# Two shift columns and one row chunk moved between stages of a conditioned convolution block on one Trainium2 core

## The chip, the cores and the metric

The kernel runs on one core of one Trainium2 chip. The metric is the device time of one execution in microseconds (us). Engines are named as in the profile: PE is the matrix engine, PEld its weight load, DVE the vector engine, ACT the scalar engine, POOL the third elementwise engine, SP the engine whose queue issues the transfers from device memory (SPq are its queue's own instructions).

## The reference, cut to what matters

One layer of a block: a modulation of the condition vector, a gated causal depthwise convolution as mixer, and an MLP with a squared ReLU. d is 2048, the sequence 256, the MLP width 8192, the convolution 31 taps.

```python
cond = jax.nn.silu(c)
mod = cond @ mod_w[i] + mod_b[i]
sh1, sc1, g1, sh2, sc2, g2 = jnp.split(mod, 6, axis=-1)
h = _rms_norm(x, norm1_g[i]) * (1.0 + sc1[:, None, :]) + sh1[:, None, :]
y = _conv_mixer(h, ...)   # in-projection to a and gt, u = a * sigmoid(gt), 31 taps per channel,
                          # layer norm over channels, silu, out-projection
x = x + (1.0 + g1[:, None, :]) * y
h = _rms_norm(x, norm2_g[i]) * (1.0 + sc2[:, None, :]) + sh2[:, None, :]
u = jnp.square(jax.nn.relu(h @ mlp_w1[i]))
x = x + (1.0 + g2[:, None, :]) * (u @ mlp_w2[i])
```

All is float32. The six modulation vectors (sh1 to g2) are a matrix-vector product with a 2048 x 12288 matrix, 96 MB of weights that are used once.

## The kernel before

**Tiling.** Channels lie on the 128 partitions in 16 tiles, tokens (256) on the free axis. The weights come in tiles of 128 x 16 x 128 float32 (1024 KB) through one ring of five buffers, the tile `raw` (RAW = 5, line 41). SP issues the loads in the order of the list `order` (lines 489 to 500), each as soon as a buffer of the ring is free (`top_up`, line 164): a load waits for the work that reads the buffer's earlier content.

**Float32 in two parts.** A weight tile is split into a rounded part `hi` (ACT, line 204) and the rest `lo` (DVE or POOL, line 207), in two halves each, by `split_w`; activations likewise by `split_act` (lines 215 to 218). `hi` and `lo` have six half buffers each, so a split also waits for the matmuls of earlier jobs. A product is hi by hi, hi by lo and lo by hi; in the last input job and in the output jobs these are three matmuls of 256 tokens (lines 228 to 230).

**Jobs.** After a first part, in which the SC1 and SH1 columns of the modulation and eight input tiles are computed together, the work is a list of jobs: `in 8` to `in 15` (one pair of tiles of a and gt each), the norm (code behind the last input job, lines 839 to 907), `out 0` to `out 7` (two output tiles each, the residual and the second norm's sums), then the MLP's `up` and `down`. The weights of a job are split one job ahead (`splits(jobs[n + 1])`, line 777), those of `out 1`'s first half already in in 15 (`parts_early`).

**Modulation beside the jobs.** What the later stages need of the modulation is computed in between, by one of two routes:

- a *row chunk* (`mod_chunk`, line 299): four matmuls on PE (line 308) with a slice of the condition as weights. 32 of them make G1 and SC2.
- a *column* (`mod_col`, line 377): DVE multiplies a weight tile of 128 x 2048 by the condition and sums along the free axis (line 388). Within out 1 to out 5 the condition has a copy in PSUM, and the column is done in two halves (line 384). 16 of them make SH2, and 16 others G2.

How many stand behind which job is written by hand in `LATE_IN` (row chunks, line 50) and `LATE_OUT` (SH2 columns, line 51). The six row chunks of in 15 are executed in the norm: the first behind the tokens' sums (`stats_end`), four behind `sum_end`, the last behind `row_end` (lines 854, 870, 896).

**Tile 14 and 15 of the convolution.** Half of the tiles' convolutions are done by DVE, tap by tap (line 622), the others by PE with diagonal weights (line 730, weights by POOL in line 715), from a shifted copy `wide` of the gated input (`copy_wide`, line 698). The copies of tiles 14 and 15 are shared between DVE (line 705, nine of them) and ACT (line 707, seven). The gate that makes their input is line 747.

**Order on an engine.** A planner places the instructions on each engine ahead of time, from the program's order, the marks of `urgent()` and its own estimate of when things are ready; `issue_after` fixes that one instruction stands behind another. On the chip each engine then works through its list in that order. ACT therefore evacuates an output job (line 916) and rounds the next job's weights (line 204) in the order that the planner chose.

Of the kernel before, what the change touches and what calls it, by code (L numbers as in the profile page):

```python
# [17 lines left out]
KT = D // P  # L18
# [16 lines left out]
SH1, SC1, G1, SH2, SC2, G2 = range(6)  # L35

GROUPS = [[4 * w + b for b in range(4)] for w in (G1, SC2)]
ROWS = [nb for g in GROUPS for nb in g]
# [8 lines left out]
COPY_AT = {8: 0, 9: 1, 10: 2, 11: 9, 12: 10, 13: 12}  # L47
PADDING = 784
UNSHIFTED = 7
LATE_IN = [0] * 8 + [4, 4, 4, 4, 4, 3, 3, 6]  # L50
LATE_OUT = [1, 2, 2, 3, 3, 3, 1, 1]
URGENT = 400
HELD = 8
EARLY_U = 5
# [10 lines left out]
def conv_block(ctx: ExitStack, tc: tile.TileContext, x, vec, dwq, c_row, mod_r, mod_c, w_first, w_in, w_out, w1, w2, out):  # L65
    nc = tc.nc
# [49 lines left out]
    state = {"used": 0}  # L116
# [12 lines left out]
    def urgent():  # L129
        return tc.high_priority(offset=URGENT)  # L130
# [89 lines left out]
    def mm(p, c, key, acts_of, ks=range(KT), merged=False):  # L220
        halves = parts[key]
        for k in ks:
            hi, lo = halves[k // HALF]
            m = acts_of[k // 2][:, k % 2, :]
            if merged:
                out_p, begin, end = p[:, c, 0:T], k == 0, k == KT - 1
                w = hi[:, k % HALF, :]
                nc.tensor.matmul(out_p, w, m[:, 0:T], start=begin, stop=False)  # L228
                nc.tensor.matmul(out_p, w, m[:, T : 2 * T], start=False, stop=False)  # L229
                state["mm_end"] = nc.tensor.matmul(out_p, lo[:, k % HALF, :], m[:, 0:T], start=False, stop=end)  # L230
                continue
            nc.tensor.matmul(p[:, c, :], hi[:, k % HALF, :], m, start=(k == 0), stop=(k == KT - 1))  # L232
            state["mm_end"] = nc.tensor.matmul(  # L233
                p[:, c, T : 2 * T], lo[:, k % HALF, :], m[:, 0:T], start=False, stop=(k == KT - 1),
                skip_group_check=True,
            )
# [62 lines left out]
    def mod_chunk(nb, kg):  # L299
        w = take(("mod", nb, kg))  # L300
        group = next(g for g in GROUPS if nb in g)
        b = group.index(nb)
        begin, end = b == 0 and kg == 0, b == len(group) - 1 and kg == 3
        if begin:
            mod_finish()
            row_ps.append(ps.tile([P, 512], F32, name="row", bufs=1))
        for k in range(4):
            state["row_end"] = nc.tensor.matmul(  # L308
                row_ps[0][32 * k : 32 * k + 32, :], cz[:, 4 * kg + k, 3 - b : 35 - b], w[:, 4 * k : 4 * k + 4, :],
                start=begin, stop=end,  # L310
            )
        if end:
            r = tmp.tile([P, 512], F32, name="rowsb", bufs=1)
            with urgent(), tc.issue_after(state["hi_end"]):
                nc.scalar.activation(r, row_ps.pop(), AF.Copy)
            pending.append(([4 * nb for nb in group], 4, r))

    def shift_row(at, w):
        if at == 0:
            row_ps.append(ps.tile([P, 512], F32, name="row", bufs=1))  # L320
        for k in range(KT):
            g = k % 4
            nc.tensor.matmul(
                row_ps[0][32 * g : 32 * g + 32, at * P : (at + 1) * P], shz[:, k, :], w[:, k, :],
                start=(k < 4), stop=(k >= KT - 4),
            )

    def fold_shift():
        n = 2 * UNSCALED
        r = tmp.tile([P, 512], F32, name="rowsb", bufs=1)  # L330
        p = ps.tile([P, 512], F32, name="row", bufs=1)
        with urgent():
            nc.scalar.activation(r[:, 0 : n * P], row_ps.pop()[:, 0 : n * P], AF.Copy)
            for j in range(n):
                nc.tensor.matmul(p[:, j : j + 1], r[:, j * P : (j + 1) * P], col("pick", 0, 1), start=True, stop=True)
            nc.scalar.activation(shc, p[:, 0:n], AF.Copy)
# [40 lines left out]
    def mod_col(at):  # L377
        w = take(("col", at)).rearrange("p k n -> p (k n)")
        which, k = divmod(at, KT)
        acc = modc[:, at : at + 1]  # L380
        if which == SH2 and "cond" in state:
            n = HALF * P
            for half, total in zip(state["cond"], (acc, rest2[:, k : k + 1])):
                nc.vector.scalar_tensor_tensor(w[:, 0:n], w[:, 0:n], 1.0, half, op0=ALU.mult, op1=ALU.mult, accum_out=total)
                w = w[:, n:]
            return
        with tc.issue_after(state["e_end"]) if "e_end" in state else ExitStack():
            nc.vector.scalar_tensor_tensor(w, w, 1.0, cb, op0=ALU.mult, op1=ALU.mult, accum_out=acc)  # L388
        if which in amps:
            return nc.vector.scalar_tensor_tensor(  # L390
                amps[which][:, k : k + 1], acc, col("modb", at), col("n1g", k), op0=ALU.add, op1=ALU.mult
            )
        elif which != SH2:
            return mod_bias(at, 1, acc)

    def mods(keys):
        for key in keys:
            if key[0] == "mod":
                mod_chunk(*key[1:])
            else:  # L400
                mod_col(key[1])
# [28 lines left out]
    def two():  # L430
        return tmp.tile([P, 2, T], F32, name="two", bufs=6)
# [28 lines left out]
        nc.scalar.activation(s, src, AF.Square)  # L460
        return s

    late = [("mod", nb, kg) for nb in ROWS for kg in range(4)] + [("col", SH2 * KT + k) for k in range(KT)]
    last = [("col", G2 * KT + k) for k in range(KT)]

    jobs = [("in", i) for i in range(KT)] + [("out", i) for i in range(HALF)]
# [2 lines left out]
    def by_tokens(job):  # L469
        return job[0] == "down" or job[0] == "up" and job[1:] not in ((0, 0), (0, 1))  # L470

    quota = {("in", i): n for i, n in enumerate(LATE_IN)}
    quota.update({("out", i): LATE_OUT[i] for i in range(HALF)})
    after = {}
    for job in jobs:
        n = quota.get(job, 0)
        after[job], late = late[:n], late[n:]
        if job[:2] in LATE_GATE:
            n = LATE_GATE[job[:2]][job[2]]
            after[job], last = last[:n], last[n:]  # L480
# [217 lines left out]
    def copy_wide(ct, both=True):  # L698
        wides[ct] = cp.tile([P, 4, T + 28], F32, name="wide", bufs=2)
        for q in range(4):  # L700
            for g in range(4):
                dst = wides[ct][32 * q : 32 * q + 32, g, :]
                src = u[ct][32 * g : 32 * g + 32, q : q + T + 28]
                if both and (g % 2 or (q, g) == (3, 2)):
                    nc.vector.tensor_copy(dst, src)
                else:
                    nc.scalar.activation(dst, src, AF.Copy)

# [62 lines left out]
    for n, job in enumerate(jobs):  # L771
# [6 lines left out]
        if n in COPY_AT:  # L778
            with tc.issue_after(state["sg"].ins) if n == HELD else ExitStack():
                copy_wide(COPY_AT[n], False)  # L780
# [3 lines left out]
        kind, i = job[0], job[-1]  # L784
# [7 lines left out]
        if job == ("up", 0, 0):  # L792
            mm(p, 0, job + (0,), xa, range(SIDE))
            for at in range(2 * UNSCALED):
                shift_row(at, shown.pop(("up", 0, at // 2, at % 2)))
            fold_shift()
            mm(p, 0, job + (0,), xa, range(SIDE, KT))
            mm(p, 1, job + (1,), xa)
        elif job in K_OUTER:
            for k2 in range(HALF):  # L800
                for c in range(2):
                    mm(p, c, job + (c,), xa if plain else hl, range(2 * k2, 2 * k2 + 2), kind == "out")
        elif kind == "in":
            rows = list(after[job]) if i < KT - 1 else []
            for c in range(2) if i < KT - 1 else (1, 0):
                for ks in (range(HALF), range(HALF, KT)):
                    mm(p, c, job + (c,), hl, ks, i == KT - 1)
                    with tc.issue_after(state["mm_end"].ins):
                        mods(rows[:1])
                    del rows[:1]  # L810
        elif by_tokens(job):
            mm_tokens(sums[kind, i // 2], job, u2 if kind == "down" else hl, n == len(jobs) - 1)
        else:
            for c in range(2):
                mm(p, c, job + (c,), hl, merged=kind == "out")
        mod_finish()
        if kind == "in":
            with urgent():
                gate(i, evac(p, out=p[:, :, 0:T]) if i < KT - 1 else p[:, :, 0:T])
                if i >= KT - 2:  # L820
                    copy_wide(i)
# [24 lines left out]
                nc.scalar.activation(sq[:, k - 12, :], cv(k), AF.Square)  # L846
            table(AF.Abs_reciprocal_sqrt, sq[:, 2, 0:1])
            sums = two()[:, 0, :]
            rows = list(after[job])
            with urgent(), tc.issue_after(state["conv_end"].ins):  # L850
                sum_round([(cv(k), sq[:, k - 12, :]) for k in (12, 13)], last=(1,))
                sum_round([(cv(14), sq[:, 2, :])], last=(0,))
# [29 lines left out]
            for k2 in range(HALF):  # L882
                e = two()
                f = ps_two()
                with urgent():
                    nc.gpsimd.tensor_tensor(e, pair_of(cvs, k2), spread(mu), op=ALU.subtract)
                    state["e_end"] = nc.vector.tensor_tensor(e, e, spread(r), op=ALU.mult).ins
                    for c in range(2):
                        k = 2 * k2 + c
# [18 lines left out]
        if kind == "out":  # L908
# [4 lines left out]
            with urgent():  # L913
                for c in range(2):
                    k = 2 * i + c
# [10 lines left out]
            for c in range(2):  # L926
                k = 2 * i + c
# [138 lines left out]
```

## Time and profile before

| what | us |
|---|---|
| median of 3 runs | 1111.2 |
| the runs | 1109.98, 1111.20, 1111.62 |
| the profiled execution, its time | 1112.2 |
| the profiled execution, its span (first to last instruction) | 1110.4 |

| engine | busy share of the span |
|---|---|
| PE | 98% |
| PEld | 81% |
| DVE | 67% |
| ACT | 46% |
| POOL | 17% |

A row of a group names the line, the engine, the operation, the tiles written and read (`out<-in`), shapes, a count after x, then busy us and the mean ns of one, then the idle time of the engine in front of them and what ended it. A row of the timeline has start and length in us, engine, line, operation, tiles, shapes, count, and in brackets the idle time before it with its releaser. Times are counted from the span's start. PE counts each float32 matmul of a row chunk and of the convolution twice, so a row chunk of four matmuls is eight instructions of line 308. Idle time of DVE, ACT or POOL costs nothing by itself, as long as PE does not wait for them.

### The profile page before, as it was taken

The numbers are of one execution on the slowest core, as the hardware profiler recorded it, in microseconds if no ns is written. First come the engines' busy times: TensorE is split into PE (matmuls) and PEld (weight loads), VectorE is DVE, ScalarE is ACT, GpSimd is POOL, SyncE is SP. The second block draws the span as 40 slices with busy tenths as digits, with TensorE's granted clock in tenths as the row PEclk, the third lists the DMA queues.
The fourth block names the chain that finished last, engine by engine and source line by source line (L and its number), as shares of the span: only waits on it lengthen the run. The fifth ranks groups of instructions, "written<-read, shape, count | busy, mean of one in ns | idle before, by whom it ended". The sixth has DMA issues, their size and how long they took to land.

```text
span 1110.4 us, 15401 instructions
## 1 busy us (share of the span) xinstructions
PE 1089.3 (98%) x6018; PEld 894.6 (81%) x6018; DVE 745.8 (67%) x1029; ACT 506.9 (46%) x677; POOL 191.7 (17%) x119
## 2 busy tenths in 40 slices
PE   7999999999899999999999999999999999999998
PEld 4888876667599998888888888888888888888887
DVE  5777789987466887666875567644656565565553
ACT  4111386754675477443444444333444344444431
POOL 0000176467679343000000000000000000000000
PEclk8999999999999999999999999999999999999999
DMA  9999989878679967878998889757888977788641
GB/s 384 421 420 422 416 335 355 339 302 344 227 304 390 395 245 252 242 233 272 374 369 290 234 242 295 299 156 261 250 237 236 248 206 226 219 241 250 209 143 38
DMA packets 142315, 314.23 MB, mean 283 GB/s; under 512 B 87585, under 2 KB 105505, under 8 KB 107297
## 3 DMA queue, kind: packets, MB, share of 16 engines
q1 hardware_dynamic: 142096, 313.11, 81.2%
q8 instruction: 47, 0.77, 0.3%
q14 instruction: 26, 0.21, 0.1%
q10 hardware_dynamic: 146, 0.13, 0.0%
HBM read 301.15 MB, written 12.07 MB: 282 GB/s over the span
## 4 chain that ended last, share of the span: by engine, by line
PE 82%; DMA 11%; DVE 4%; SPq 1%; ACT 1%; issue 0%; DVEq 0%; ACTq 0%
PE mm L256 18%; PE mm L257 18%; PE mm L255 18%; DMA raw<-mod_c 9%; PE mm L232 6%; PE mm L233 3%; DVE raw L388 3%; PE acc L230 2%; PE acc L228 2%; PE acc L229 2%; PE row L308 2%; PE mm L730 2%; DMA flat<-two 1%; PE mm L229 1%; SPq L275 1%; DVE lo L207 1%
## 5 line engine op out<-in xcount | busy, mean ns | idle before, releaser
L204 ACT ACTIVATE hi<-raw 128x1024 fp32r<-128x1024 f32 x320 | 333.7, 1056 | 359.7 <-PE mm L257 292.8
L207 DVE TENSOR_TENSOR lo<-raw,hi 128x1024 fp32r<-128x1024 f32 x257 | 311.7, 1222 | 168.4 <-ACT hi L204 168.1
L256 PE MATMUL mm<-lo,u 128*128 128x512 f32 x496 | 193.2, 390 | 0.4 <-DVE lo L207 0.4
L255 PE MATMUL mm<-hi,u 128*128 128x512 f32 x496 | 193.0, 389 | 0.0
L257 PE MATMUL mm<-hi,u 128*128 128x512 f32 x496 | 193.0, 389 | 0.0
L207 POOL TENSOR_TENSOR lo<-raw,hi 128x1024 fp32r<-128x1024 f32 x63 | 152.3, 2445 | 206.3 <-DMA raw<-w_in 132.3
L257 PE MATMUL mm<-hi,hl 128*128 128x512 f32 x480 | 186.7, 389 | 0.0
L256 PE MATMUL mm<-lo,hl 128*128 128x512 f32 x480 | 186.7, 389 | 0.0
L255 PE MATMUL mm<-hi,hl 128*128 128x512 f32 x480 | 186.7, 389 | 0.0
L388 DVE SCALAR_TENSOR_TENSOR raw<-raw,cond 128x2048 f32<-128x2048 f32 x49 | 114.5, 2339 | 51.9 <-DMA raw<-mod_c 51.9
L256 PEld LDWEIGHTS mm<-lo,u 128*128 128x128 f32 x496 | 93.1, 188 | 20.2 <-DVE lo L207 1.2
L257 PEld LDWEIGHTS mm<-hi,u 128*128 128x128 f32 x496 | 93.1, 188 | 19.3
L255 PEld LDWEIGHTS mm<-hi,u 128*128 128x128 f32 x496 | 93.1, 188 | 19.0
L256 PEld LDWEIGHTS mm<-lo,hl 128*128 128x128 f32 x480 | 90.1, 188 | 18.8
L257 PEld LDWEIGHTS mm<-hi,hl 128*128 128x128 f32 x480 | 90.1, 188 | 18.7
L255 PEld LDWEIGHTS mm<-hi,hl 128*128 128x128 f32 x480 | 90.1, 188 | 18.6
L622 DVE SCALAR_TENSOR_TENSOR acc<-u,v,acc 128x256 f32<-128x256 f32 x224 | 94.5, 484 | 1.9
L232 PE MATMUL mm<-hl,hi 128*128 128x512 f32 x224 | 81.7, 405 | 0.0
L557 PE MATMUL mm<-two,first 128*128 128x256 f32 x256 | 61.0, 393 | 8.1 <-ACT two L588 8.1
L228 PE MATMUL acc<-hl,hi 128*128 128x256 f32 x224 | 64.2, 287 | 1.6 <-ACT hi L204 1.6
L230 PE MATMUL acc<-hl,lo 128*128 128x256 f32 x224 | 64.2, 287 | 0.8 <-DVE lo L207 0.8
L557 PEld LDWEIGHTS mm<-two,first 128*128 128x128 f32 x256 | 50.0, 197 | 17.5 <-ACT two L588 10.5
(183 smaller groups left out, 1287.3 us busy)
## 6 DMA issues: line engine op xcount, KB each, us to landing
raw<-w SPq DMA_DIRECT2D x128, 1024.0 KB, 5.5
raw<-mod_c SPq DMA_DIRECT2D x62, 1024.0 KB, 10.4
raw<-mod_r SPq DMA_DIRECT2D x32, 1024.0 KB, 7.8
raw<-w_in SPq DMA_DIRECT2D x16, 1024.0 KB, 7.1
raw<-w_out SPq DMA_DIRECT2D x16, 1024.0 KB, 7.7
first<-w_first SPq DMA_DIRECT2D x15, 1024.0 KB, 17.2
flat<-two SPq DMA_DIRECT2D x30, 256.0 KB, 2.8
two<-flat SPq DMA_DIRECT2D x120, 64.0 KB, 4.4
```

The costliest lines, as they stand in the source:

```text
L204: state["w_hi"] = nc.scalar.activation(hi, w[:, ks, :], AF.Copy).ins
L207: end = by.tensor_tensor(lo, w[:, ks, :], hi.bitcast(F32), op=ALU.subtract)
L228: nc.tensor.matmul(out_p, w, m[:, 0:T], start=begin, stop=False)
L229: nc.tensor.matmul(out_p, w, m[:, T : 2 * T], start=False, stop=False)
L230: state["mm_end"] = nc.tensor.matmul(out_p, lo[:, k % HALF, :], m[:, 0:T], start=False, stop=end)
L232: nc.tensor.matmul(p[:, c, :], hi[:, k % HALF, :], m, start=(k == 0), stop=(k == KT - 1))
L255: nc.tensor.matmul(p, p_hi, hi, start=begin, stop=False)
L256: nc.tensor.matmul(p, p_hi, lo, start=False, stop=False)
L257: nc.tensor.matmul(p, p_lo, hi, start=False, stop=end)
L388: nc.vector.scalar_tensor_tensor(w, w, 1.0, cb, op0=ALU.mult, op1=ALU.mult, accum_out=acc)
L557: step = nc.tensor.matmul(held[n][:, c, :], w[:, 2 * n + c, :], h, start=k == 0 and c == 0, stop=k == KT - 1, skip_group_check=True)
L622: nc.vector.scalar_tensor_tensor(out, s, w, acc, op0=ALU.mult, op1=ALU.add)
```

## The change

Two of the sixteen SH2 columns (`cols_in`, k = 0 and 1) are taken from the list of the output stage and put in front of in 15's row chunks, in the order of the loads as in the order of execution. They are emitted in front of in 15's matmuls, with an ordering that puts them behind the last DVE copy of tile 14 (`state["copied"]`). In 14 has two row chunks instead of three, in 15 seven instead of six; of these five, instead of four, stand in the middle group of the norm. The columns of out 0 to out 7 become 1, 1, 2, 2, 3, 3, 1, 1 instead of 1, 2, 2, 3, 3, 3, 1, 1. What is computed is the same.

```diff
-LATE_IN = [0] * 8 + [4, 4, 4, 4, 4, 3, 3, 6]
-LATE_OUT = [1, 2, 2, 3, 3, 3, 1, 1]
+LATE_IN = [0] * 8 + [4, 4, 4, 4, 4, 3, 2, 7]
+LATE_OUT = [1, 1, 2, 2, 3, 3, 1, 1]
+COLS_IN = 2
...
-    late = [("mod", nb, kg) for nb in ROWS for kg in range(4)] + [("col", SH2 * KT + k) for k in range(KT)]
+    late = [("mod", nb, kg) for nb in ROWS for kg in range(4)] + [("col", SH2 * KT + k) for k in range(COLS_IN, KT)]
+    cols_in = [("col", SH2 * KT + k) for k in range(COLS_IN)]
...
         after[job], late = late[:n], late[n:]
+        if job == ("in", KT - 1):
+            after[job] = cols_in + after[job]
...
                 if both and (g % 2 or (q, g) == (3, 2)):
-                    nc.vector.tensor_copy(dst, src)
+                    state["copied"] = nc.vector.tensor_copy(dst, src).ins
...
             rows = list(after[job]) if i < KT - 1 else []
+            if i == KT - 1:
+                state["e_end"] = state["copied"]
+                mods(cols_in)
...
-            rows = list(after[job])
+            rows = after[job][COLS_IN:]
```

## The prediction

> **What bounds the kernel now.** I read the waits of TensorE first, then busy time by stretches, then the timelines of the engines around the change. Columns of the first fence: who waited for whom, us in total, times, longest. The stretches are from:to, length, busy us of each engine with its instruction count in brackets, granted clock, DMA share, GB/s; the last three are of PE alone.
>
> ```profile
> span 1110.4 us, 15401 instructions
> ```
> ```profile
> PE acc L228 <- ACT hi L204: 1.6, 1, 1.6
> PE mm L228 <- ACT hl L215: 1.4, 1, 1.4
> PE mm L229 <- DVE hl L218: 1.2, 2, 0.8
> PE acc L230 <- DVE lo L207: 0.8, 1, 0.8
> ...
> PE mm L228 <- DVE hl L217: 0.3, 1, 0.3
> ```
> ```profile
> 275.00:290.00 15.00, 14.91 (x175) 11.74 (x178) 5.44 (x12) 9.03 (x16) 8.41 (x4) 1.00 0.41 139
> 290.00:308.00 18.00, 15.13 (x144) 9.72 (x134) 10.24 (x19) 13.12 (x25) 10.72 (x10) 1.00 0.74 290
> 308.00:340.00 32.00, 31.97 (x265) 31.56 (x264) 22.42 (x34) 21.88 (x33) 26.10 (x12) 1.00 0.83 318
> 340.00:386.00 46.00, 46.00 (x385) 45.93 (x383) 34.02 (x53) 23.02 (x36) 28.40 (x18) 1.00 0.99 389
> ```
> ```profile
> 374.70:386.10 11.40, 11.40 (x96) 1.00 1.01 423
> 386.10:394.00 7.90, 5.54 (x32) 0.78 0.80 300
> 390.00:393.00 3.00, 3.00 (x16) 0.50 0.68 205
> ```
>
> TensorE sets the time: it is busy through the last input job (275 to 290) and through the output stage (308 to 386). From the input jobs to the end of the output stage it idles at two places only: in the norm (1.4 + 1.2 + 0.3 us, 290 to 308) and once in front of the last output job (1.6 + 0.8 us, behind 386). So the change can win in three ways: by taking matmuls out of a stretch where PE is full, by filling the norm's hole, and by removing the second hole.
>
> That second hole costs more than its 2.4 us of idle time. A whole job is 96 matmuls in 11.40 us, 0.119 us each. Between 386.1 and 394.0 PE did 32, which at that pace is 3.8 us, in 7.9 us: **4.1 us are lost**. The part beyond the idle time is the clock: in 390 to 393 the granted clock is 0.50.
>
> The Trainium skill, "TensorE: Matmul & The Clock Gate", section on HAM oscillation, has as its rule that idle gaps over about 3.4 us are to be avoided. By that rule gaps of 1.6 and 0.8 us would leave the clock alone, the hole would be worth its 2.4 us, and rival C below would be the result. The trace does not agree: 0.50 stands right behind these short gaps.
>
> **Why that hole is there.** ScalarE's timeline at the place, the issue of the two loads on SP, and the time to landing by the page:
>
> ```profile
> 386.18 0.54 ACT L916 ACTIVATE acc<-acc,gb,modc 128x256 f32<-128x256 f32 x1 [5.99 <-PE acc L230]
> 386.64 1.99 ACT L204 ACTIVATE hi<-raw 128x1024 fp32r<-128x1024 f32 x2
> 388.53 0.53 ACT L916 ACTIVATE acc<-acc,gb,modc 128x256 f32<-128x256 f32 x1
> 388.98 2.00 ACT L204 ACTIVATE hi<-raw 128x1024 fp32r<-128x1024 f32 x2
> ```
> ```profile
> 372.49 2.75 SPq L185 DMA_DIRECT2D raw<-w_out  x2
> ```
> ```profile
> raw<-w_out SPq DMA_DIRECT2D x16, 1024.0 KB, 7.7
> ```
>
> The weights of out 7 were issued by 375.2 (372.49 + 2.75) and at the usual 7.7 us lay in place by about 383. Yet their rounding (L204) began at 386.64, because it is queued behind the evacuation L916 of out 6, which waited 5.99 us for that job's matmuls. Then one L204 takes 1 us, the low part on DVE follows it (the wait of 0.8), and PE stands. L204 of the next job has the higher priority in the code (splits come first, both urgent), so the planner put it second only because by its own plan the load was not there yet; and as it stands between the two L916 of one job, in the plan it missed by no more than about one L916, 0.5 us.
>
> **The change, part by part.**
>
> (a) One row chunk leaves in 14 for the norm. PE's timeline, one chunk in in 14 and the five at the norm:
>
> ```profile
> 263.87 1.06 PE L308 MATMUL row<-raw,cz 128*32 128x512 f32 x8
> ```
> ```profile
> 295.69 4.50 PE L308 MATMUL row<-raw,cz 128*32 128x512 f32 x40
> ```
>
> Five chunks in 4.50 us: 0.9 us each. PE is full in the input jobs, so in 14 and all behind it come 0.9 us earlier: **-0.9**. In the norm there are now seven chunks; the sixth fills the 1.4 us that PE waits for the first rounded pair, if its load is there. The seventh is loaded last, into a buffer that the second frees. SP today, by the loads that follow one another there (start, length, line, tiles, count), and the landing times of all weight loads:
>
> ```profile
> 261.93 32.23 SPq L185 DMA_DIRECT2D raw<-mod_r  x6
> ```
> ```profile
> 296.81 0.33 SPq L185 DMA_DIRECT2D raw<-w_out  x1
> ```
> ```profile
> 298.53 1.19 SPq L185 DMA_DIRECT2D raw<-w_out  x2
> ```
> ```profile
> DMA to landing us min/median/max: 4.7/6.8/18.2
> ```
>
> The second chunk's buffer comes free at 296.81, where out 1's weights are issued today. With the shortest landing time (only one other load is in flight) the chunk is there at 301.5 and done at 302.4. PE reaches that point at 300.2 (295.69 + 4.50) and starts the first pair after its 1.4 us, at 301.6. The pair is pushed by 0.8 us, and the waits behind it (0.3, and the two for L218, 1.2) take that up: **0**. If the load takes the median 6.8 us instead, the chunk is done at 304.5; the pair is pushed by 2.9 us, of which the waits take 1.5: bound +1.4. No gain is possible, since this is added work. I take 0, nearer to the row of an idle queue.
>
> (b) Two shift columns run on DVE in in 15, behind the copies of tile 14. DVE and POOL there, and the only column that ran beside POOL:
>
> ```profile
> 267.26 5.72 DVE L705 COPY wide<-u 32x284 f32<-32x284 f32 x9
> 274.93 0.42 DVE L669 TENSOR_TENSOR cv<-cv,small 128x256 f32<-128x256 f32 x1 [1.95 <-PE small L675]
> 283.92 0.48 DVE L747 SCALAR_TENSOR_TENSOR u<-mm,v,two 128x256 f32<-128x256 f32 x1 [8.57 <-ACT two L745]
> 284.44 4.27 DVE L705 COPY wide<-u 32x284 f32<-32x284 f32 x9
> ```
> ```profile
> 268.61 1.97 POOL L715 TENSOR_TENSOR diag<-v,dwq_sb 128x1024 f32<-128x1024 f32 x1
> 273.85 2.39 POOL L207 TENSOR_TENSOR lo<-raw,hi 128x1024 fp32r<-128x1024 f32 x1 [3.27 <-ACT hi L204]
> 277.91 2.40 POOL L207 TENSOR_TENSOR lo<-raw,hi 128x1024 fp32r<-128x1024 f32 x1 [1.67 <-ACT hi L204]
> 280.73 2.39 POOL L207 TENSOR_TENSOR lo<-raw,hi 128x1024 fp32r<-128x1024 f32 x1 [0.42 <-ACT hi L204]
> 283.61 2.39 POOL L207 TENSOR_TENSOR lo<-raw,hi 128x1024 fp32r<-128x1024 f32 x1 [0.49 <-ACT hi L204]
> ```
> ```profile
> 314.21 4.25 DVE L388 SCALAR_TENSOR_TENSOR raw<-raw,cond 128x2048 f32<-128x2048 f32 x1
> ```
> ```profile
> 313.90 6.83 POOL L207 TENSOR_TENSOR lo<-raw,hi 128x1024 fp32r<-128x1024 f32 x2 [7.50 <-ACT hi L204]
> ```
> ```profile
> L388 DVE SCALAR_TENSOR_TENSOR raw<-raw,cond 128x2048 f32<-128x2048 f32 x49 | 114.5, 2339 | 51.9 <-DMA raw<-mod_c 51.9
> ```
>
> A column is 2.34 us by itself. DVE is free from 273.0 (267.26 + 5.72) to 283.92 but for 0.42 us, so 4.7 us fit. The loads stand where two row chunks stand today, from 261.93 on, with one chunk fewer ahead; at 6.8 us they land near 269 to 272, before DVE is free. Beside POOL both slow down: at 314.21 the column took 4.25 instead of 2.34, and POOL's two splits 6.83 instead of 4.78, so an overlap costs each about 2 us. Both columns then end by 273.0 + 2 x 4.25 = 281.5 at worst, ahead of the gate L747, and nothing urgent is queued behind them.
>
> What is late next is POOL. From 273.85 on DVE has 3.85 us of column left (4.7 less 0.85). Sharing evenly, the first split ends at 278.6; the second shares until 281.5 and ends at 282.5 instead of 280.3; third and fourth follow without gaps and end at 287.3 instead of 286.0. The fourth matters: nine copies of tile 15 took 4.27 us beside it, and the nine of tile 14, beside a split and the diagonal, took 5.72, so POOL's work holds them up. They end 1.3 us later at most, and PE's convolution of tile 15 waits for them. It is less if the diagonal (268.61), whose two splits now load one place earlier, leaves sooner and the columns start sooner: about 0.4 us. The other bound is a gain: a fourth split clear of the copies would give back what the convolution loses, seen against that of tile 14:
>
> ```profile
> 287.73:292.19 4.46, 4.46 (x64) 1.00 0.51 209
> 264.76:268.40 3.64, 3.63 (x64) 1.00 1.01 421
> ```
>
> 4.46 - 3.64 = 0.8. So -0.8 to +1.3; I take **+0.6**, since the contended row is the nearest.
>
> (c) The output stage loses two column loads and their DVE work in out 1 and out 3, and the buffer queue gains one row chunk ahead of out 1's second half. DMA is the tight thing there: share 0.99 at 389 GB/s in 340 to 386, that is 2.7 us for 1024 KB; in 275 to 290 the share is 0.41, so two loads have room. At out 7's weights the net is one load less, 2.7 us sooner. The plan missed by some 0.5 us, so the rounding of out 7 goes ahead of L916 and runs when its load lands, some 3 us before PE wants it: **-4.1**. If the order stays, 0. I take -4.1, because the planner counts the same loads.
>
> Sum: -0.9 + 0 + 0.6 - 4.1 = **-4.4 us**. On the profiled span that is 1110.4 to 1106.0; that execution took 1112.2 (1.8 us outside the span), 1.0 above the median of the runs, so on the median 1111.2 - 4.4 = **1106.8**.
>
> **The rivals.**
>
> B, the order stays: the plan's load was later than I infer, or the limit in the plan is buffers. For it: the order is fixed before the chip runs, and no row shows the plan. Then -0.9 + 0.6: **1110.9**, with the hole still in front of out 7.
>
> C, the hole goes, but usual runs never paid the half clock. Its price is 4.1 - 2.4 = 1.7 us, and the three runs of before lie 1.6 us apart (1109.98 to 1111.62). Then -0.9 + 0.6 - 2.4 = -2.7: **1108.5**. The rule of the Trainium skill named above ("TensorE: Matmul & The Clock Gate", HAM oscillation) would end here too.
>
> D, slower: a hole of the same kind opens early in the output stage while the late one stays. The place is out 2, whose weights (issued at 298.53) now have one more row chunk ahead of them, 2.7 us, and are only relieved later. It decides when their planned landing passes the planned end of out 0 or out 1; then an L916 goes ahead of the rounding there, and the price is again 4.1: -0.3 + 4.1, **1115.0**. Against it: the trace has no wait of PE there, and the stage starts 0.3 us sooner.
>
> **How the numbers follow.** My forecast 0.48, with a range of its own from 1105.4 (-0.9 - 0.8 - 4.1) to 1108.9 (-0.9 + 1.3 + 1.4 - 4.1); C 0.10, B 0.17, D 0.25. A difference under 0.2%, 2.2 us, can't be told from none. A and C are faster by more, 0.58; B is the same, 0.17; D is slower, 0.25. The range reaches from a little under A's low end, 1104.8, over B and into the cheaper half of D, 1114.5; what is left out is the rest of D and a little below.
>
> **What would show it.** (a) PE has two chunks in in 14 instead of three, in 15 starts 0.9 us sooner, and 56 L308 records stand at the norm. (b) Two L388 with cond on DVE between the two groups of copies, each between 2.3 and 4.3 us; POOL's last split ends up to 1.3 us nearer the end of the copies. (c) The first L204 of out 7 stands ahead of out 6's L916, PE has no wait at acc L228, and the granted clock is 1.00 there. I am wrong if L916 still comes first, if a new wait of PE at L228 or L230 turns up in out 1 to out 6, or if PE waits longer than 1 us for the copies of tile 15.

## The result, and the profile after

| | median, us | runs |
|---|---|---|
| before | 1111.20 | 1109.80 to 1111.62 (6) |
| after | 1106.57 | 1106.42 to 1106.74 (6) |

The ratio is 0.9961, 95% interval 0.9948 to 0.9974: 4.6 us faster, against 4.4 forecast. The profiled spans are 1110.4 and 1104.8, which is 5.6 apart; the profiled execution of before was 1.0 us above its median, so the stages below are read from the profiles and the total from the medians. Part of that 1.0 us lies where the change touches nothing: at about 526 us, in `up`, the profiled execution of before has a wait of PE that the one of after has not.

```profile
PE mm L256 <- DVE lo L207: 0.4, 1, 0.4
```

One inserted line moves the line numbers by one, further down by four to seven (L204 is L205 now, L916 is L923).

The waits of PE after the change (who waited for whom, us in total, times, longest), then ScalarE and PE at the place of the old hole (PE: stretch, length, busy with count, clock, DMA):

```profile
PE row L309 <- DMA raw<-mod_r: 1.5, 1, 1.5
PE mm L230 <- DVE hl L219: 0.8, 1, 0.8
...
PE acc L734 <- DVE wide L709: 0.4, 1, 0.4
```
```profile
378.17 3.89 ACT L205 ACTIVATE hi<-raw 128x1024 fp32r<-128x1024 f32 x4
385.83 1.11 ACT L923 ACTIVATE acc<-acc,gb,modc 128x256 f32<-128x256 f32 x2 [3.77 <-PE acc L231]
```
```profile
384.80:392.70 7.90, 7.90 (x68) 1.00 1.01 373
```

All four roundings of out 7 now stand ahead of out 6's evacuations and are done by 382, and PE runs through: 68 matmuls in a stretch of 7.9 us, where it did 32 before in one as long, at a clock of 1.00. The 36 more are worth 36 x 0.119 = 4.3 us. The loads of out 7 were issued sooner, too, within 367.30 to 371.26 instead of 372.49 to 375.24:

```profile
367.30 3.96 SPq L186 DMA_DIRECT2D raw<-w_out  x2
```

Around in 15 and the norm, DVE first, then POOL, then PE:

```profile
267.41 4.56 DVE L709 COPY wide<-u 32x284 f32<-32x284 f32 x9
272.00 2.29 DVE L389 SCALAR_TENSOR_TENSOR raw<-raw,cond 128x2048 f32<-128x2048 f32 x1
...
274.22 4.49 DVE L389 SCALAR_TENSOR_TENSOR raw<-raw,cond 128x2048 f32<-128x2048 f32 x1
...
283.01 0.48 DVE L751 SCALAR_TENSOR_TENSOR u<-mm,v,two 128x256 f32<-128x256 f32 x1 [3.96 <-ACT two L749]
283.53 4.83 DVE L709 COPY wide<-u 32x284 f32<-32x284 f32 x9
...
292.10 0.48 DVE L744 TENSOR_SCALAR cv<-acc,v 128x256 f32<-128x256 f32 x1 [3.22 <-PE small L679]
```
```profile
273.01 3.54 POOL L208 TENSOR_TENSOR lo<-raw,hi 128x1024 fp32r<-128x1024 f32 x1 [3.45 <-ACT hi L205]
277.00 8.65 POOL L208 TENSOR_TENSOR lo<-raw,hi 128x1024 fp32r<-128x1024 f32 x3 [0.44 <-ACT hi L205]
```
```profile
295.34 4.50 PE L309 MATMUL row<-raw,cz 128*32 128x512 f32 x40
301.38 1.07 PE L309 MATMUL row<-raw,cz 128*32 128x512 f32 x8 [1.54 <-DMA raw<-mod_r]
302.38 0.39 PE L229 MATMUL mm<-hl,hi 128*128 128x256 f32 x1
...
305.05 0.39 PE L230 MATMUL mm<-hl,hi 128*128 128x256 f32 x1 [0.81 <-DVE hl L219]
```

The gate of tile 15 starts at 283.01 instead of 283.92: 0.91 us is the row chunk. Nine copies take 4.83 instead of 4.27, and tile 15's result follows at 292.10 instead of 292.44: of the 0.91 us, 0.56 are given back to the columns. In the norm the last chunk waits 1.54 us for its load, and out 6 is evacuated at 385.83 instead of 386.18, 0.35 earlier: the norm cost nothing more.

### The profile page after: what moved, and what is told of

Its sections match the earlier page's. It is cut to its first block, busy times and chain, and to the rows that moved or that the text cites. A ratio compares the mean times of both kernels' runs of the same rounds, so it can differ in the third digit from the quotient of the medians.

```text
span 1104.8 us, 15399 instructions
## 1 busy us (share of the span) xinstructions
PE 1087.2 (98%) x6018; PEld 893.3 (81%) x6018; DVE 746.3 (68%) x1025; ACT 507.6 (46%) x677; POOL 195.0 (18%) x119
## 4 chain that ended last, share of the span: by engine, by line
PE 87%; DMA 9%; DVE 3%; ACT 1%; issue 0%; SPq 0%; ACTq 0%
PE mm L257 20%; PE mm L256 20%; PE mm L258 20%; DMA raw<-mod_c 8%; PE mm L233 6%; PE mm L234 3%; PE acc L231 2%; PE acc L230 2%; PE acc L229 2%; PE row L309 2%; DVE raw L389 2%; PE mm L734 2%; PE mm L230 1%; DMA x<-x 1%; PE mm L231 1%; PE mm L229 1%
## 5 line engine op out<-in xcount | busy, mean ns | idle before, releaser
L205 ACT ACTIVATE hi<-raw 128x1024 fp32r<-128x1024 f32 x320 | 334.4, 1057 | 367.7 <-PE mm L258 301.8
L208 POOL TENSOR_TENSOR lo<-raw,hi 128x1024 fp32r<-128x1024 f32 x63 | 156.8, 2516 | 198.1 <-ACT hi L205 198.1
L389 DVE SCALAR_TENSOR_TENSOR raw<-raw,cond 128x2048 f32<-128x2048 f32 x51 | 120.7, 2369 | 49.3 <-DMA raw<-mod_c 49.2
L229 PE MATMUL acc<-hl,hi 128*128 128x256 f32 x224 | 63.4, 283 | 0.0
L230 PE MATMUL acc<-hl,hi 128*128 128x256 f32 x224 | 63.4, 283 | 0.0
```

The costliest lines, as they stand in the source:

```text
L205: state["w_hi"] = nc.scalar.activation(hi, w[:, ks, :], AF.Copy).ins
L208: end = by.tensor_tensor(lo, w[:, ks, :], hi.bitcast(F32), op=ALU.subtract)
```

## The experiments

All are timed against runs of the kernel before on the same chip (medians 1111.0 to 1111.4). They ran on four chips, so differences between rows of up to 0.4 us mean little.

| | median, us | ratio to before, 95% interval |
|---|---|---|
| e1, row chunk alone | 1111.91 | 1.0004, 0.9995 to 1.0013 |
| e2, columns alone | 1107.83 | 0.9974, 0.9964 to 0.9984 |
| e3, ScalarE's order alone | 1107.57 | 0.9972, 0.9961 to 0.9982 |
| e4, changed kernel, old order | 1113.90 | 1.0028, 1.0018 to 1.0037 |
| e5, order and row chunk | 1110.59 | 0.9998, 0.9989 to 1.0008 |
| e6, fourth split later in POOL's list | 1106.73 | 0.9967, 0.9958 to 0.9977 |
| e7, order, out 7's column to out 2 | 1109.91 | 0.9996, 0.9987 to 1.0006 |
| e8, second column in DVE's gap | 1105.98 | 0.9967, 0.9952 to 0.9982 |
| e9, that, and fourth split on DVE | 1106.69 | 0.9961, 0.9946 to 0.9975 |
| e10, changed, two columns left out | 1106.02 | 0.9953, 0.9938 to 0.9968 |
| e11, e5 with out 7's low parts on POOL | 1110.48 | 0.9990, 0.9980 to 0.9999 |
| e12, fourth split on DVE, columns first | 1105.46 | 0.9955, 0.9941 to 0.9969 |

**The two parts alone (e1, e2).**

```diff
 e1, on the kernel before
-LATE_IN = [0] * 8 + [4, 4, 4, 4, 4, 3, 3, 6]
+LATE_IN = [0] * 8 + [4, 4, 4, 4, 4, 3, 2, 7]
 e2, on the changed kernel
-LATE_IN = [0] * 8 + [4, 4, 4, 4, 4, 3, 2, 7]
+LATE_IN = [0] * 8 + [4, 4, 4, 4, 4, 3, 3, 6]
```

> The kernel before with the row chunk moved (three and two chunks become three, two and seven) and no column moved. Theory: the chunk is worth -0.9, and the hole in front of out 7 stays, because all four roundings of out 7 stand behind out 6's evacuation in ScalarE's list; that list has them behind both evacuations instead of one, which costs up to 0.5 more: 1110.3 to 1110.8. Rival, the chunk's shift alone also ends the hole: 1106.2.

> The changed kernel with the row chunk put back into in 14: the two columns alone are moved. Theory: without the chunk's -0.9, with +0.6 for the columns and -4.1 for the hole: 1107.5, no wait of PE in front of out 7. Rival, the hole went because of the chunk: 1111.8.

ScalarE in e1 at the place of the hole:

```profile
385.43 1.11 ACT L916 ACTIVATE acc<-acc,gb,modc 128x256 f32<-128x256 f32 x2 [6.50 <-PE acc L230]
386.46 1.99 ACT L204 ACTIVATE hi<-raw 128x1024 fp32r<-128x1024 f32 x2
```
```profile
PE acc L228 <- ACT hi L204: 2.2, 1, 2.2
```

With the chunk alone the rounding of out 7 stands behind both evacuations, as expected, and the wait grew from 1.6 to 2.2 us. That alone does not bring the time to 1111.9, over the range expected, since the low part's wait fell from 0.8 to 0.5 us and the two together grew by 0.3. But behind them the clock of PE is 0.50 for twice as long as in before, through the whole of 388 to 394:

```profile
388.00:394.00 6.00, 5.54 (x26) 0.50 0.85 320
```

Five of the eleven runs lie at 1110.8 to 1111.0, at the upper end of the range or just over it, and six at 1111.9 or more, among them the profiled one. That the longer half clock is what parts them is likely, and not shown. With the columns alone the roundings stand ahead of both evacuations, there is no wait in front of out 7, and the time is 1107.8:

```profile
381.44 3.88 ACT L205 ACTIVATE hi<-raw 128x1024 fp32r<-128x1024 f32 x4
388.56 1.11 ACT L923 ACTIVATE acc<-acc,gb,modc 128x256 f32<-128x256 f32 x2 [3.23 <-PE acc L231]
```

So the columns end the hole, and the chunk without them is worth nothing in the total.

**The order alone, and the order put back (e3, e4).** In e4 out 7's splits are called between the two evacuations of out 6 and fixed behind the first.

```diff
 e3, on the kernel before
                 for c in range(2):
                     k = 2 * i + c
-                    nc.scalar.activation(t2[:, c, :], t2[:, c, :], AF.Identity, scale=mcol(G1, k), bias=gb[:, k : k + 1])
+                    with tc.issue_after(state["w_hi"]) if i == HALF - 2 else ExitStack():
+                        nc.scalar.activation(t2[:, c, :], t2[:, c, :], AF.Identity, scale=mcol(G1, k), bias=gb[:, k : k + 1])
 e4, on the changed kernel
-        if n < len(jobs) - 1:
+        if n < len(jobs) - 1 and job != ("out", HALF - 2):
             splits(jobs[n + 1])
...
+                    if i == HALF - 2 and c == 0:
+                        state["evacuated"] = first.ins
+                        splits(jobs[n + 1])
```

> The kernel before with one ordering added: out 6's evacuations stand behind out 7's roundings on ScalarE. No load, column or chunk is moved. Theory, the hole is a matter of that order alone: -4.1, 1107.1, granted clock 1.00 there. Rival, the hole comes from late loads or a busy DVE, and the columns' leaving removed it: no gain, 1111. Rival, the half clock is not paid in usual runs: -2.4, 1108.8.

> The changed kernel with out 7's roundings forced behind out 6's first evacuation, as they stood before. Theory: the hole comes back with its half clock, +4.1: 1110.7. Rival, the relieved loads matter and not the order: no loss, 1106.6. Rival, only the idle time costs: +2.4, 1109.0.

PE in e3 over the hole, the first rounding of out 7 on ScalarE, and what PE waits for (the first two of the waits are the norm's); then ScalarE in e4, e4's waits, and its stretches:

```profile
384.80:392.70 7.90, 7.90 (x68) 1.00 1.00 403
```
```profile
382.75 2.01 ACT L204 ACTIVATE hi<-raw 128x1024 fp32r<-128x1024 f32 x2 [3.41 <-DMA raw<-w_out]
```
```profile
PE mm L228 <- ACT hl L215: 1.4, 1, 1.4
PE mm L229 <- DVE hl L218: 1.2, 2, 0.8
PE mm L232 <- DVE u L218: 1.1, 2, 0.9
```
```profile
385.75 0.54 ACT L924 ACTIVATE acc<-acc,gb,modc 128x256 f32<-128x256 f32 x1 [7.55 <-PE acc L232]
386.21 3.89 ACT L206 ACTIVATE hi<-raw 128x1024 fp32r<-128x1024 f32 x4
```
```profile
PE mm L234 <- DVE u L220: 2.2, 1, 2.2
PE acc L230 <- ACT hi L206: 1.6, 1, 1.6
...
PE acc L232 <- DVE lo L209: 1.0, 2, 0.8
```
```profile
386.00:389.00 3.00, 0.93 (x5) 1.00 0.21 85
389.00:392.00 3.00, 2.79 (x24) 1.00 0.14 16
405.00:408.00 3.00, 0.80 (x5) 0.99 0.18 74
408.00:411.00 3.00, 3.00 (x30) 0.50 0.02 5
```

No load, column or chunk is moved in e3, and the hole is gone: again 68 matmuls in 7.9 us. The rounding there waits for its load until 382.75, about the 383 read for before, so it is not the sooner loads that end the hole but the order. That shows its cause. But the time fell by 3.7 from that chip's 1111.24, not by 4.1: at the start of up 0 PE now waits for the last activations (L218 on DVE), which the hole had covered. Putting the old order into the changed kernel brings back the waits of 1.6 and 0.8 us, but the time rose by 7.3 instead of 4.1, because more is late behind the hole: in DVE's list the low parts stand ahead of the last activations (L220), for which PE waits 2.2 us at up 0, and a half clock follows. So e4 shows that the order brings the hole back, not what it alone costs.

**Order and chunk without the columns (e5, e7, e11).** e5 is e3 with e1's line; e7 is e3 with `LATE_OUT = [1, 2, 3, 3, 3, 3, 1, 0]`; e11 is e5 with ("out", 7) in `POOLED`.

> The kernel before with the added ordering (out 6's evacuations behind out 7's roundings) and the row chunk moved; all sixteen columns stay in the output stage. Theory, the parts add up: 1107.6 (ordering alone) less 0.7, 1106.9, with the waits of PE for DVE L218 at the start of up 0 left as in the ordering alone (1.3 us). Rival, the columns' leaving brings nothing beyond the order: 1106.6 or less and no such waits.

> The kernel before with the added ordering and the column of out 7 moved to out 2 (1, 2, 3, 3, 3, 3, 1, 0). Theory, the waits that the ordering alone leaves at the start of up 0 come from columns at the end of DVE's list in the output stage: they go, 1.3 less than the ordering alone: 1106.3. Rival, they come from the last job's own chain of evacuation, norm and splits: 1107.6 as the ordering alone.

> The kernel with the added ordering and the moved row chunk (1110.6, with 1.6 us of PE waiting for DVE's low part of out 7's weights, and 1.7 us of waits at the start of up 0), and now out 7's low parts done by POOL, which is idle there. Theory, what is left of the hole is DVE's list, in which five columns' halves stand ahead of the low parts: both groups of waits go, 1110.6 less 3.3, 1107.3. Rival, the loads of out 7 come too late with sixteen columns in the stage, or the waits at up 0 come from elsewhere: 1108.9 to 1110.6.

Both sides were wrong in e5: 1110.6. Its waits, and DVE in front of out 7's low parts (each row of L384 is one half column; four stand between 381.10 and 385.78, and the first and the last are shown):

```profile
PE mm L232 <- DVE u L218: 1.6, 2, 1.4
PE acc L230 <- DVE lo L207: 1.6, 1, 1.6
```
```profile
381.10 1.21 DVE L384 SCALAR_TENSOR_TENSOR raw<-raw,mm 128x1024 f32<-128x1024 f32 x1
...
384.53 1.22 DVE L384 SCALAR_TENSOR_TENSOR raw<-raw,mm 128x1024 f32<-128x1024 f32 x1
...
385.89 4.63 DVE L207 TENSOR_TENSOR lo<-raw,hi 128x1024 fp32r<-128x1024 f32 x4
```

and the same place in the changed kernel:

```profile
379.48 1.22 DVE L385 SCALAR_TENSOR_TENSOR raw<-raw,mm 128x1024 f32<-128x1024 f32 x1
...
381.31 4.62 DVE L208 TENSOR_TENSOR lo<-raw,hi 128x1024 fp32r<-128x1024 f32 x4
```

The rounding is ahead of the evacuations in e5 and begins at 380.60 (378.17 in the changed kernel), but the low part stands behind half columns on DVE until 385.89, some 4.6 us later than in the changed kernel, and PE waits 1.6 us for it. In e7 it is the same wait (1.6 us for DVE lo L207), while the waits at up 0 are gone, as expected; the total of 1109.9 missed the forecast, most likely for the first reason. In e11 POOL did the low parts, at 3.1 us each; the wait of 1.6 us became three of at most 0.7, 1.5 together, those at up 0 stayed (1.5 us for L218), and the total did not move beyond the intervals. (The profiled execution of e11 is the slowest of its ten, 1113.59, so its waits may be more than the usual.) So a job's split stands in two lists, ScalarE's and DVE's, and both have to be early. Taking two columns out of the stage does both at once; the order of ScalarE alone does it only where DVE's list happens to be right, as in e3.

**What the columns cost in in 15 (e6, e8, e9, e10, e12).** In e6 the low part of the second half of `parts_early` is emitted behind tile 15's copies, on POOL; in e9 and e12 on DVE behind tile 14's result (`cv14`); in e8 and e9 the second column is called there too. e10 leaves the two columns out and fills them with ones.

```diff
 e8 and e9
-                mods(cols_in)
+                mods(cols_in[:1])
...
+            state["e_end"] = state["cv14"]
+            mods(cols_in[1:])
 e6, e9 and e12, in split_w
+                if key in parts_early and h == 1:
+                    state["put_off"] = lo, w[:, ks, :], hi
+                    halves.append((hi, lo))
+                    continue
 e12, behind tile 14's result
+            lo, w, hi = state.pop("put_off")
+            with tc.issue_after(state["cv14"]):
+                nc.vector.tensor_tensor(lo, w, hi.bitcast(F32), op=ALU.subtract)
```

> The changed kernel with POOL's fourth split in in 15 (second half of out 1's early weights) put behind tile 15's copies on DVE. Theory, that split holds up the copies: the nine copies take about 3 instead of 4.8 us, PE's convolution of tile 15 3.6 instead of 4.5, and the time falls by 0.8 to 1.2: 1105.4 to 1105.8. Rival, the copies are held by something else or the norm's late row chunk takes the gain up: 1106.6.

> The changed kernel with the second column put behind tile 14's result on DVE (the 3.2 us in which DVE waits for the convolution of tile 15) instead of directly behind the first. Theory, the columns' cost comes from POOL being slowed by the second one, which delays its last split into the copies: the copies take 4.3 instead of 4.8 and the time falls by 0.5: 1106.1. Rival, the later buffer release delays the norm's row chunks and costs as much or more: 1106.6 to 1107.5.

> The kernel with the second column in DVE's gap, and the low part of the fourth split of in 15 done by DVE in that gap too, instead of by POOL before it. Theory, POOL's fourth split is what still holds up tile 15's copies: the nine copies fall from 4.25 to about 2.8 us, the wait inside the convolution of tile 15 goes, and the time falls by 0.5 to 0.8 from 1105.98: 1105.2 to 1105.5. Rival, ScalarE's seven copies or the norm's late row chunk bound it: 1106.0.

> The changed kernel with the two columns neither loaded nor computed anywhere (two of the sixteen SH2 columns are filled with ones instead). Theory, the columns in in 15 cost 0.6 and their leaving the output stage is what ends the hole: no wait of PE in front of out 7, and 0.6 less than the changed kernel: 1106.0. Rival, the cost is in the later loads of the norm's row chunks: the wait of 1.5 us for the last chunk goes as well and the time is 1105.0 or less.

> The changed kernel, both columns ahead of the gate as in it, with the low part of the fourth split of in 15 done by DVE behind tile 14's result instead of by POOL. Theory: with the fourth split gone from POOL the copies take 2.85 us although the second column still slows POOL; the buffer of the second column is free at 278.7 as in the changed kernel, so of the norm's row chunks only the last one waits (1.2 to 1.6 us) and the norm's start stays 1.5 earlier than in the changed kernel: 1105.1 to 1105.4, the fastest. Rival, out 1's buffer, freed 2.3 us later, makes a second row chunk late: 1106.0 to 1106.7.

e6 did not do what it was meant to: its last split on POOL ran at 283.24, as soon as POOL was free, since the copies run on another engine and nothing made POOL wait for them. It decides nothing. e8, its copies:

```profile
283.50 4.25 DVE L709 COPY wide<-u 32x284 f32<-32x284 f32 x9
```

They are back at 4.25, and the profiled span is 0.6 us shorter than that of the changed kernel (1104.2 against 1104.8), as the medians are (1105.98 against 1106.57): the second column beside POOL is what the columns cost. The total alone would not show it: one of the five runs took 1109.1, and the intervals of the ratios overlap. e10 agrees, with copies of 4.26 us and 1106.02 without the columns' work. e9 and e12, copies and waits, and PE behind the norm in e9:

```profile
283.49 2.85 DVE L713 COPY wide<-u 32x284 f32<-32x284 f32 x9
```
```profile
PE row L313 <- DMA raw<-mod_r: 3.5, 2, 2.1
```
```profile
304.00:308.00 4.00, 4.00 (x23) 0.57 0.97 418
```
```profile
283.33 2.85 DVE L713 COPY wide<-u 32x284 f32<-32x284 f32 x9
```
```profile
PE row L313 <- DMA raw<-mod_r: 1.6, 1, 1.6
```

In both, with POOL's fourth split gone, the copies take 2.85 us. In the profiled execution of e9 (1107.49) that came to nothing: two row chunks of the norm wait for their loads, 3.5 us together, since two buffers of the ring are freed late, and behind them the clock is 0.57 for 4 us. The waits are near what the rival said; the clock nobody forecast. The four runs of e9 lie 2.5 us apart (1105.75 to 1108.28), so its median says little. In e12 only one chunk waits, 1.6 us as in the changed kernel, and the time is 1105.46 (1105.06 to 1105.96), just over the range expected and the fastest median of all; the intervals of the ratios of e12 and of the changed kernel overlap, the ranges of their runs do not.

## Why the prediction was right

**(a), -0.9:** measured -0.91 at the gate of tile 15. The last chunk's load came at the time worked out (301.38 against 301.5), the first pair was pushed from 301.58 to 302.38, and the waits behind it took that up.

**(b), +0.6:** measured +0.56, and e8 gives the same by another way. That POOL's fourth split holds up the copies is shown by e9 and e12, where they take 2.85 us without it. But +0.6 was picked between -0.8 and +1.3 and not worked out, so its closeness is in part luck, and the working of the upper bound had the wrong mechanism: the two engines do not share evenly, they take turns. The first column, begun at 272.00, took its full 2.29, and the split begun at 273.01 ended at 276.55, which is one split's time behind the column's end; the second column (274.22) took 4.49, one column's time behind that split; the next split, begun at 277.00, follows it. The Trainium skill has it so ("SBUF — State Buffer", section on the two separate sides): where a DVE instruction reads two inputs from SBUF, as the column does, and a POOL instruction reads SBUF, the port that they share is locked for a whole instruction and the other one blocks. The trace agrees with it. From the times of before, the end of the fourth split comes out at 287.3 under both readings, so the bound did not suffer.

**(c), -4.1:** measured 4.3 in the profile by the count of matmuls, and e3 shows that the order in ScalarE's list was the cause. The loads of out 7 came 4 to 5 us sooner by their issue, not 2.7, so that step was too small; by e3 the sum does not hang on it. That the plan's own load time decided the order was an inference, and stays one: no run shows the plan's times. What was incomplete is that DVE's list is a second condition, which e5 and e7 showed, and that the columns' leaving also covers the waits at up 0 that e3 laid bare. Rival D's mechanism, a split late in a list at another place, did not occur in the changed kernel, but e5, e7 and e11 show that it is near.

**Rival C**, that usual runs do not pay the half clock, does not fit most runs. Of the first 25 runs of before beside the experiments, 4 lie at 1109.6 to 1110.0 and the rest from 1111.0 up. The mean granted clock of each run was recorded: the three at 1.000 took 1109.58 to 1110.02, and the five at 0.998 took 1111.24 to 1112.22. A stretch of 3.4 us at 0.50, as in the trace of before behind the hole (390.2 to 393.6), lowers the mean over 1110 us by 0.0015. (The others, at 0.992 to 0.997, can't be read so: a half clock in the first part, as in before's trace at 18 to 25 us, lowers the mean too.) So the price is near 1.5 us, as rival C has it (1.7), and most runs pay it; where in those runs the stretch lies is not shown, as only one execution of each kernel was profiled. Against the runs of before that do not pay, the change gains about 3 us and not 4.6. Nor are two groups always the clock: e3's runs lie at 1107.0 to 1107.6 and 1108.9 to 1109.1, and both groups hold runs at 1.000.

## What to carry to other kernels

When the matrix engine stands idle for weights whose load has long landed, look at what is queued ahead of their preparation in the same engine's list: an evacuation that waits for the matrix engine blocks the preparation of the next job's weights. Every engine that prepares them has such a list, and work that can move to an idle stretch (here two columns of DVE and their loads) shortens more than one of them at once. What such a move costs sits at the next shared resource, here POOL's turn in front of the copies and the ring's buffers; e12, which gets around the first, has a median 1.1 us lower.

## What the runs showed of the hardware

Idle time of the same length on PE does not always cost clock. In before, waits of 1.6 and 0.8 us were followed by a granted clock of 0.50; in e4 the same waits at the same place, with one of 0.2 beside them, left it at 1.00 (24 matmuls from 389 to 392), and a later wait of 2.2 us was followed by 0.50. In e2 the norm's waits of 1.4 and 1.0 us were followed by 0.5 for some 7 us; in before and in e3 the same 1.4, with 1.2 and 0.3 behind it, cost no clock. The two stretches of e2:

```profile
304.00:308.00 4.00, 3.38 (x15) 0.52 0.98 418
308.00:311.00 3.00, 3.00 (x16) 0.51 1.01 426
```

The Trainium skill ("TensorE: Matmul & The Clock Gate", Part 1) has activity windows of 3.4 us that run freely, so that a change of clock depends on where in a window it falls. These rows agree with that; with the rule in its section on HAM oscillation, that gaps over about 3.4 us are to be avoided, they do not, as shorter ones were followed by a lower clock here.
